# One product order for the tall Strassen-Winograd sets, weight sums into the first block, and x read back on SyncE's queue

## The chip, the cores and the metric

The kernel runs on 1 core of one Trainium2 chip. Times are device microseconds (us). The engines are PE (TensorE, matrix products), ACT (ScalarE), DVE (VectorE), POOL (GpSimd) and SP (SyncE, which here only issues transfers). A share or a wait comes from one profiled execution; the median comes from runs without a profile.

## The reference

One block on x of 512 x 1024 in fp32: a gated feed-forward layer, a mixer, a second feed-forward layer and a norm.

```python
def swiglu(x, w_gu, w_down):
    g, u = jnp.split(x @ w_gu, 2, axis=-1)
    return (jax.nn.silu(g) * u) @ w_down
...
    # mixer, h is the normed x
    z = h @ w_in        # parts cb, cc, cu, q, k, v, g_lr, r, ga, gb
    y_conv = (cb * causal_short_conv(cc * cu, conv_w)) @ w_out_conv
    ...                 # o: gated linear attention of q, k, v, normed by head
    y_gla = (o.astype(h.dtype) * jax.nn.silu(r)) @ w_out_gla
    merged = jax.nn.sigmoid(ga) * y_conv + jax.nn.sigmoid(gb) * y_gla
    return merged @ w_o
...
        x = x + 0.5 * swiglu(rmsnorm(x, norm_ffn1_g[l]), ffn1_w_gu[l], ffn1_w_down[l])
        x = x + hybrid_mixer(rmsnorm(x, norm_mix_g[l]), w_in[l], ...)
        x = x + 0.5 * swiglu(rmsnorm(x, norm_ffn2_g[l]), ffn2_w_gu[l], ffn2_w_down[l])
    return rmsnorm(x, final_norm_g)
```

The hidden width of the feed-forward layers is 2816, which is 22 tiles of 128.

## The kernel before

Every product is done in three passes on split operands: a weight block `f` (128 x 1024 fp32) is cast by ACT to a high part `wh` (L387), DVE subtracts it from the block for the low part `wl` (L388), and PE adds op_high·wh, op_high·wl and op_low·wh. The activations are split in the same way into `op`. Three `wh`, three `wl`, fourteen `op` and ten `f` buffers go round.

Most of the large products use the Strassen-Winograd scheme, seven half-size products for eight, named m1, p2, p5, q6, q7, p4 and p3. The weight block of each is a sum of the four quarters a11, a12, a21, a22. The sums are made in the quarters' own buffers: POOL issues transfers that add one buffer to another (`add`, L354), and DVE does the sum that is called s3 (L381 in tall sets, L366 in the narrow ones). Two kinds of sets use the scheme. A narrow "set" has one weight block for each product. A "tall" set has the inner dimension in two halves, s = 0 and 1, with four quarters each, so it has fourteen steps of twelve 128x512 products (L711). In the SP order, a tall set's quarters are loaded as a11, a21, a22, a12.

A tall set has three pairs of PSUM banks: b takes m1, q6, q7 and p4 one upon another, a starts as a copy of m1 and takes p2, c takes p5 and then p3. What is needed of a sum on the way is copied out after the product's second half: in a feed-forward tall, ACT takes p2 through Silu (L831), p5 (L834), and copies q6 (L837); DVE takes q7 (L839). q7 adds into b, so it can't start before the copy of q6 is done. The first step of the set that follows a tall is put ahead of that tall's p3, and takes the pair a as soon as p2 was read.

The order of the products of a tall is a list. TALL_ORDER is m1, p5, q6, p2, q7, p3, p4; FIRST is m1, p5, p2, q6, q7, p3, p4. The tall sets are, in the order of time: ffn1 up at f = 4, 8, 12 (TALL_ORDER) and 16 (FIRST), each f being the first of four tiles of the hidden width; in the mixer v, ga, gb (TALL_ORDER) and "out", the product with w_out_conv (FIRST); ffn2 up at f = 0 (FIRST), 6, 10, 14, 18 (TALL_ORDER); two of ffn2's down product (DOWN_ORDER). PE's order is that of the code. A scheduler sets the order on the other engines; a step's weights are issued two steps ahead of its products.

In ffn1 and ffn2, sixteen small ACT copies for each of some tall sets (L880, 32x512, from `z` into `hid`) turn the finished tile; they stand between the casts.

Ahead of the last part of the mixer, the attention's output O has been split into operands (L1757, L1758). Then come the two halves e = 0 and 1 of the product with w_out_gla (L459 to L461, eight weight blocks each), and w_o. The gates ga and gb lie in device memory and come back by SP tile by tile (L1770), followed by a sigmoid on ACT (L1771). x, which was written to `xs` earlier, is read back into the buffer that O had (X2), by eight transfers that POOL issues (L1797); w_o's evacuation adds it. SP also issues all weight loads (L350), in one order.

The kernel starts with fp32 products of a 128x128 tile of ones (L283), WARM of them, whose result is not used, each run by PE in two passes.

Of the kernel before, what the change touches and what calls it, by code (L numbers as in the profile page):

```python
# [12 lines left out]
ALU = mybir.AluOpType  # L13
ENG = mybir.EngineType

P = 128
S = 512
D = 1024
KD = D // P
DFF = 2816  # L20
KF = DFF // P
# [13 lines left out]

V_G1, V_GM, V_G2, V_GLA, V_CONV, V_GB = 0, 8, 16, 24, 32, 56
NVEC = 60
WARM = 8
ODD_FILL = 272

TAIL = 4
# [84 lines left out]
LATE = []  # L126
# [5 lines left out]

TALL_ORDER = ("m1", "p5", "q6", "p2", "q7", "p3", "p4")
DOWN_ORDER = ("m1", "p2", "q6", "p5", "q7", "p3", "p4")
FIRST = ("m1", "p5", "p2", "q6", "q7", "p3", "p4")
TALL = {}
ORDERS = {}


def tall(name, mat, cols, base=0, order_=TALL_ORDER):  # L140

    ORDERS[name] = order_

    firsts = []
    for s in range(2):
        firsts.append(len(PLAN))
        TALL[len(PLAN)] = name, s
        PLAN.extend((mat, base + 4 * j + 2 * s, 2, (c,), 512) for c in cols for j in range(2))
    STEPS.extend((n, p) for p in order_ for n in firsts)
# [14 lines left out]
def up_plan(up, plain, slow):  # L164

    kinds = ["tall"] * ((KF - plain) // 4)
    kinds.insert(len(kinds) if slow else 1, "set")
    f = plain
    for kind in kinds:
        if kind == "tall":  # L170
            edge = f == KF - 6 if slow else f == 0
            tall((up, f), up, (f * P, DFF + f * P), order_=FIRST if edge else TALL_ORDER)
        else:
            at = len(STEPS)
            sets(up, [(f * P, DFF + f * P)])
            LATE.append(STEPS[-1][0])
            STEPS[at - 4 : at + 1] = [STEPS[at], *STEPS[at - 4 : at]]
        UPS.setdefault(up, []).append((kind, f))
        f += 4 if kind == "tall" else 2
# [24 lines left out]
def mixer_plan():  # L204
    units(group("w_in", KD, (QO, KO, QO + P, KO + P)))
    for h in (2, 3):
        units(single("w_in", KD, QO + h * P))
        units(single("w_in", KD, KO + h * P))
    for name, col in (("v", VO), ("ga", GA), ("gb", GB)):
        tall(name, "w_in", (col, col + 512))  # L210
    at = len(STEPS)
    base = {"cb": CB, "r": RO}
    sets("w_in", [(CC + i * HW, CU + i * HW) if n == "conv" else
                  (base[n] + 2 * i * HW, base[n] + (2 * i + 1) * HW) for n, i in MSETS])
    LATE.append(STEPS[-1][0])
    STEPS[at - 2 : at + 2] = [STEPS[at], *STEPS[at - 2 : at], STEPS[at + 1]]
    tall("out", "w_out_conv", (0, 512), order_=FIRST)
    for e in range(2):
        units(wide("w_out_gla", KD, 512 * e))
    units(group("w_o", KD, (0, P, 2 * P, 3 * P)))  # L220
    for d in range(4, KD):
        units(single("w_o", KD, d * P))
    ENDS.append(len(STEPS))
# [13 lines left out]
def block_kernel(ctx: ExitStack, tc: tile.TileContext, xT, vecs, gf, gup, wgl, wts, out):  # L237
    nc = tc.nc
# [54 lines left out]
    x = [XS[0][:, k] for k in range(KD)]  # L293
# [3 lines left out]
    class Weights:  # L297
# [58 lines left out]
        def issue(self):  # L356
            at = self.issued
            self.fetch(at)
            new = self.loads.get(at, ())
            raw = {(n, i): self.dma(n + i) for i in ((0, 2, 3, 1) if new and new[0] in TALL else range(4))  # L360
                   for n in new}
            self.raw.update((n, [raw[n, i] for i in range(4)]) for n in new)
            for n in self.sums.get(at, ()):
                self.raw[n].append(tile_of("f", [P, 1024]))
                a11, a12, a21, a22, s3 = self.raw[n]
                nc.vector.tensor_tensor(out=s3, in0=a11, in1=a21, op=ALU.add)  # L366
                self.add(a21, a22)
            for n in self.firsts.get(at, ()):
                self.add(self.raw[n][2], self.raw[n][3])
            for n in self.pre.get(at, ()):  # L370
                self.raw[n] = self.dma(n)
            n, p = STEPS[at]
            w = unit_cols(PLAN[n])
            if p is None:
                raw = self.raw[n]
            else:
                a11, a12, a21, a22, s3 = (self.raw[n] + [None])[:5]
                if n in TALL:
                    if p == "q7":
                        s3 = a11 if ORDERS[TALL[n][0]] == FIRST else a21  # L380
                        nc.vector.tensor_tensor(out=s3, in0=a11, in1=a22, op=ALU.subtract)  # L381
                raw = {"m1": a11, "p2": a12, "q6": a11, "p5": a21, "q7": s3, "p4": a22,
                       "p3": a11 if n in LATE else a12}[p]
            late = at >= len(STEPS) - TAIL
            h = tile_of("op" if late else "wh", [P, 1024], F32R)
            l = tile_of("op" if late else "wl", [P, 1024], F32R)
            nc.scalar.copy(h[:, :w], raw[:, :w])  # L387
            nc.vector.tensor_tensor(out=l[:, :w], in0=raw[:, :w], in1=h[:, :w].bitcast(F32),  # L388
                                    op=ALU.subtract)
            if p == "m1":  # L390
                self.add(a11, a21)
            if n in LATE:
                if p == "q6":
                    self.add(a11, a12)
            elif p == "p2":
                self.add(a12, a11)
            self.issued += 1
            self.ready.append((h, l))
# [398 lines left out]
    def begin_weighed(hid, norm):  # L797
        f = KF - KD
        for k in range(KD):
            nc.scalar.activation(hid[:, f + k], x[k], AF.Copy, scale=norm.g(k))  # L800
        return Operands(lambda j, l: hid[:, f + 4 * j : f + 4 * j + 4, l * HW : (l + 1) * HW],
                        FIRST)

    def ffn(up, down, norm, nxt, plain, at):
        hid = tile_of("hid", [P, KF, S])
# [464 lines left out]
    def mixer(norm, nxt):  # L1270
        xh, xl = norm.h, norm.l
        cpool = pools["small"]
        xs = dram.tile([KD, P, S], F32, tag="xs", name="xs")
# [338 lines left out]
        def split_o(h):  # L1612
            for a, b in split_pair(O[h]):
                og_h.append(a)
                og_l.append(b)
# [21 lines left out]
            (4, "q6"): [lambda: output(3)], (4, "p3"): [lambda: squares(3)],  # L1637
            (5, "q7"): [lambda: normalise(0)], (5, "p3"): [lambda: normalise(1)],
            (6, "q7"): [lambda: normalise(2)], (6, "p3"): [lambda: normalise(3)],
            ("out", 1, "q6"): [lambda: co.make("p4")], ("out", 0, "q7"): [lambda: split_o(0)],  # L1640
            ("out", 1, "q7"): [lambda: split_o(1)], ("out", 0, "p3"): [lambda: split_o(2)],
            ("out", 1, "p3"): [lambda: split_o(3)],
        }
# [146 lines left out]

        def between(e):
            def extra(k):
                if e == 1 and k == 3:
                    XS.append(big("X2"))
                    x[:] = [XS[-1][:, k] for k in range(KD)]
                    for k_ in range(KD):
                        nc.gpsimd.dma_start(x[k_], xs[k_])  # L1797
                if k in (1, 3, 4, 6):
                    t = (1, 3, 4, 6).index(k)
                    mul(m[e][t], m[e][t], gate("ga", t, e))  # L1800
                if e == 1 and k in (5, 6):
                    turned(2 * (k - 5))
            return extra
# [95 lines left out]
```

## Time and profile before

| | before |
|---|---|
| median of 3 runs | 1164.95 us (1162.81 to 1165.26) |
| profiled execution | 1166.64 us |
| its span, first to last instruction | 1164.9 us |
| mean granted TensorE clock | 0.995 |
| PE busy | 1148.0 us |
| DVE, ACT, POOL busy | 895.5, 714.6, 160.3 us |
| moved by DMA | 203.20 MB, mean 174 GB/s |

The span leaves out what lies around the first and the last instruction. A busy share is an average over all stages; the rows below are of single stages. In a row of the trace stand the start, the time, the engine, the line, the operation, out<-in, and the number of instructions; the bracket gives the engine's idle time ahead of it and what ended it.

### The profile page before, as it was taken

Reading aid. Unit: us, or ns where it says so; the run is one execution under the profiler, and the core shown is the slowest. Engines: PE = TensorE matmul, PEld = TensorE weight load, DVE = VectorE, ACT = ScalarE, POOL = GpSimd, SP = SyncE. Lnnn points to the kernel's source line nnn. Section 1 sums busy time; section 2 is a strip of 40 time slices with the busy share of each in tenths; the row PEclk is TensorE's granted clock in tenths of the full one; section 3 lists DMA queues with packets and bytes.
Section 4 is the critical chain, followed back from the end, with each engine's and each line's share of the span. In section 5 each row is a group of like instructions: output and inputs, shape, how many; then the busy total and the mean of one; then the engine's idle time right before and its main releaser. Section 6 shows DMA issues by size and latency. Waiting matters only on the chain.

```text
span 1164.9 us, 16337 instructions
## 1 busy us (share of the span) xinstructions
PE 1148.0 (99%) x6280; PEld 997.7 (86%) x6280; DVE 895.5 (77%) x1061; ACT 714.6 (61%) x923; POOL 160.3 (14%) x199
## 2 busy tenths in 40 slices
PE   9999998999999999999999999999999999999997
PEld 7888787989998888889999998788889878888886
DVE  7986765898887975767797999455876776799966
ACT  6568767755553756665665567524668587665543
POOL 0011111001121010111011112000110464111100
PEclk9999998999999999999999999999999999999999
DMA  9476696557674285788576787834576856877711
GB/s 362 109 198 136 175 246 149 165 135 189 163 217 154 55 237 137 205 235 229 134 172 147 197 205 195 304 109 127 121 170 153 233 145 154 228 202 181 178 55 73
DMA packets 59869, 203.20 MB, mean 174 GB/s; under 512 B 6960, under 2 KB 7088, under 8 KB 59792
## 3 DMA queue, kind: packets, MB, share of 16 engines
q0 software_dynamic: 20288, 73.41, 33.5%
q1 hardware_dynamic: 36912, 124.04, 30.5%
q10 hardware_dynamic: 2592, 4.72, 1.1%
q8 instruction: 49, 0.80, 0.3%
q14 instruction: 28, 0.23, 0.1%
HBM read 124.55 MB, written 8.39 MB: 114 GB/s over the span
## 4 chain that ended last, share of the span: by engine, by line
PE 87%; ACT 6%; DVE 3%; DMA 2%; issue 1%; SPq 0%; ACTq 0%; DVEq 0%
PE mm L711 39%; PE mm L624 24%; PE mm L442 6%; PE mm L420 3%; PE mm L419 3%; PE mm L418 3%; ACT wh L387 3%; ACT hid L880 2%; DVE wl L388 1%; PE mm L460 1%; PE mm L461 1%; PE mm L459 1%; DMA tp<-ga 1%; PE mm L1161 1%; PE mm L1159 1%
## 5 line engine op out<-in xcount | busy, mean ns | idle before, releaser
L388 DVE TENSOR_TENSOR wl<-f,wh 128x1024 fp32r<-128x1024 f32 (+1 forms) x349 | 425.0, 1222 | 172.4 <-ACT wh L387 167.6
L387 ACT CAST wh<-f 128x1024 fp32r<-128x1024 f32 (+1 forms) x349 | 364.4, 1048 | 308.8 <-PE mm L711 103.5
L711 PE MATMUL mm<-wh,op 128*128 128x512 f32 x1680 | 526.3, 392 | 4.7 <-ACT tp L837 3.9
L711 PEld LDWEIGHTS mm<-wh,op 128*128 128x128 f32 x1680 | 316.9, 189 | 71.7 <-ACT tp L837 4.8
L711 PE MATMUL mm<-wl,op 128*128 128x512 f32 x840 | 329.4, 392 | 3.6 <-DVE wl L388 3.3
L624 PE MATMUL mm<-op,wh 128*128 128x256 f32 x1456 | 263.2, 284 | 0.0
L354 POOL DMA_DIRECT2D f<-f x132 | 113.9, 868 | 874.7 <-DVE wl L388 416.4
L624 PEld LDWEIGHTS mm<-op,wh 128*128 128x128 f32 x1456 | 227.6, 192 | 0.7
L624 PE MATMUL mm<-op,wl 128*128 128x256 f32 x728 | 206.3, 283 | 0.0
L711 PEld LDWEIGHTS mm<-wl,op 128*128 128x128 f32 x840 | 158.5, 189 | 39.6 <-DVE wl L388 7.5
L624 PEld LDWEIGHTS mm<-op,wl 128*128 128x128 f32 x728 | 139.6, 192 | 0.0
L880 ACT COPY hid<-z 32x512 f32<-32x512 f32 x112 | 69.2, 618 | 2.8 <-DVE z L874 1.1
L682 ACT CAST op<-hid 128x1024 fp32r<-128x1024 f32 x42 | 44.0, 1050 | 20.3 <-PE mm L711 11.2
L683 DVE TENSOR_TENSOR op<-hid,op 128x1024 fp32r<-128x1024 f32 x42 | 51.1, 1220 | 4.4 <-ACT op L682 4.2
L419 PE MATMUL mm<-op,wh 128*128 128x512 f32 x132 | 51.4, 390 | 0.0
L418 PE MATMUL mm<-op,wh 128*128 128x512 f32 x132 | 51.4, 390 | 0.0
L420 PE MATMUL mm<-op,wl 128*128 128x512 f32 x132 | 51.4, 389 | 0.0
L442 PE MATMUL mm<-op,wh 128*128 128x512 f32 x192 | 48.9, 397 | 0.4 <-DVE op L491 0.4
L381 DVE TENSOR_TENSOR f<-f,f 128x1024 f32<-128x1024 f32 x30 | 37.9, 1269 | 12.9 <-DMA f<-f 6.6
L442 PEld LDWEIGHTS mm<-op,wh 128*128 128x128 f32 x192 | 36.6, 192 | 8.3 <-ACT wh L387 0.6
L1059 POOL COPY X<-hid 32x512 f32<-32x512 f32 x32 | 33.2, 1038 | 1.3
L419 PEld LDWEIGHTS mm<-op,wh 128*128 128x128 f32 x132 | 24.8, 188 | 5.1
(331 smaller groups left out, 1192.5 us busy)
## 6 DMA issues: line engine op xcount, KB each, us to landing
f<-wts SPq DMA_DIRECT2D x219, 512.0 KB, 4.9
f<-f POOLq DMA_DIRECT2D x132, 512.0 KB, 5.2
xs<-X POOLq DMA_DIRECT2D x8, 256.0 KB, 4.4
ga<-tp ACTq DMA_DIRECT2D x8, 256.0 KB, 6.0
gb<-tp ACTq DMA_DIRECT2D x8, 256.0 KB, 5.1
tp<-ga SPq DMA_DIRECT2D x8, 256.0 KB, 5.4
X<-xs POOLq DMA_DIRECT2D x8, 256.0 KB, 7.9
tp<-gb SPq DMA_DIRECT2D x8, 256.0 KB, 5.3
```

The costliest lines, as they stand in the source:

```text
L354: nc.gpsimd.dma_start(out_, a, accum_op=ALU.add)
L387: nc.scalar.copy(h[:, :w], raw[:, :w])
L388: nc.vector.tensor_tensor(out=l[:, :w], in0=raw[:, :w], in1=h[:, :w].bitcast(F32), op=ALU.subtract)
L418: nc.tensor.matmul(o, wh, ah, start=first, stop=False)
L419: nc.tensor.matmul(o, wh, al, start=False, stop=False)
L420: nc.tensor.matmul(o, wl, ah, start=False, stop=last)
L442: nc.tensor.matmul(o[c], w[:, s : s + P], a[k], start=k == 0 and j == 0, stop=k == kt - 1 and j == 2)
L624: nc.tensor.matmul(to, ww[:, s], aa[:, t], start=fresh and k == 0 and e == 0 and j == 0, stop=k == 3 and j == 2, skip_group_check=True)
L682: nc.scalar.copy(hv, v)
L683: nc.vector.tensor_tensor(out=lv, in0=v, in1=hv.bitcast(F32), op=ALU.subtract)
L711: nc.tensor.matmul(self.bank[b][e], aa[:, c], ww, start=fresh and i == 0 and n == 0, stop=k == 3 and n == 2, skip_group_check=True)
L880: nc.scalar.copy(dst[:, :, :, 32 * a : 32 * (a + 1)], src[:, :, :, 32 * q : 32 * (q + 1)])
```

## The change

It has four parts. WARM goes from 8 to 10. FIRST is gone, and the three tall sets that had it use TALL_ORDER, with one hook of "out" moved so that the operand of p4 is still made after the fourth product. In tall sets of TALL_ORDER (`soon`), the subtraction s3 = a11 − a22 is issued at q6 instead of at q7 and always goes into a21, the transfer a11 += a12 is issued behind q6 in place of a12 += a11 behind p2, and p3 reads a11 instead of a12; the down product's tall sets now put s3 into a11. x is read back by SP, one tile with each weight block of w_out_gla's second half.

```diff
-WARM = 8
+WARM = 10
...
-FIRST = ("m1", "p5", "p2", "q6", "q7", "p3", "p4")
...
-            edge = f == KF - 6 if slow else f == 0
-            tall((up, f), up, (f * P, DFF + f * P), order_=FIRST if edge else TALL_ORDER)
+            tall((up, f), up, (f * P, DFF + f * P))
...
-    tall("out", "w_out_conv", (0, 512), order_=FIRST)
+    tall("out", "w_out_conv", (0, 512))
...
                 a11, a12, a21, a22, s3 = (self.raw[n] + [None])[:5]
+                soon = n in TALL and ORDERS[TALL[n][0]] == TALL_ORDER
                 if n in TALL:
-                    if p == "q7":
-                        s3 = a11 if ORDERS[TALL[n][0]] == FIRST else a21
+                    s3 = a21 if soon else a11
+                    if p == "q7" and not soon:
                         nc.vector.tensor_tensor(out=s3, in0=a11, in1=a22, op=ALU.subtract)
                 raw = {"m1": a11, "p2": a12, "q6": a11, "p5": a21, "q7": s3, "p4": a22,
-                       "p3": a11 if n in LATE else a12}[p]
+                       "p3": a11 if soon or n in LATE else a12}[p]
...
             if p == "m1":
                 self.add(a11, a21)
-            if n in LATE:
+            if p is not None and (soon or n in LATE):
                 if p == "q6":
+                    if soon:
+                        nc.vector.tensor_tensor(out=s3, in0=a11, in1=a22, op=ALU.subtract)
                     self.add(a11, a12)
             elif p == "p2":
                 self.add(a12, a11)
...
-            ("out", 1, "q6"): [lambda: co.make("p4")], ("out", 0, "q7"): [lambda: split_o(0)],
+            ("out", 1, "p2"): [lambda: co.make("p4")], ("out", 0, "q7"): [lambda: split_o(0)],
...
-                if e == 1 and k == 3:
+                if e == 1 and k == 0:
                     XS.append(big("X2"))
                     x[:] = [XS[-1][:, k] for k in range(KD)]
-                    for k_ in range(KD):
-                        nc.gpsimd.dma_start(x[k_], xs[k_])
+                if e == 1:
+                    tc.keep_in_program_order(nc.sync.dma_start(x[k], xs[k]))
```

ACT's order at ffn1 f = 16, before. mm234 and mm235 are the banks b, with q6, and mm240 and mm241 the banks a, with p2; f213 and f221 are a11 of the two halves, here holding s3 of q7.

```order
L831 ACTIVATE tp258_1558<-mm240_1468 128x512
L880 COPY hid20_188<-z229_1390 32x16x32
L831 ACTIVATE tp259_1560<-mm241_1469 128x512
L387 CAST wh260_1565<-f213_1298 128x1024
L880 COPY hid20_188<-z229_1390 32x16x32 x2
L387 CAST wh263_1587<-f221_1343 128x1024
L880 COPY hid20_188<-z229_1390 32x16x32
L837 COPY tp265_1603<-mm234_1430 128x512
L837 COPY tp266_1605<-mm235_1431 128x512
```

The same place after (L838 is L837 of before, L832 is L831, L386 is L387, and L881 is L880; f214 and f222 are a21):

```order
L838 COPY tp258_1562<-mm234_1432 128x512
L881 COPY hid20_190<-z229_1392 32x16x32
L838 COPY tp259_1564<-mm235_1433 128x512
L386 CAST wh260_1568<-f214_1302 128x1024
L881 COPY hid20_190<-z229_1392 32x16x32 x2
L386 CAST wh263_1589<-f222_1347 128x1024
L881 COPY hid20_190<-z229_1392 32x16x32
L832 ACTIVATE tp265_1605<-mm240_1470 128x512
L832 ACTIVATE tp266_1607<-mm241_1471 128x512
```

The copies of q6 and the evacuation of p2 have changed places; the casts of q7's two halves stand between them as before.

DVE's order in the same tall, from the split of p5's second half on, before (f213 to f216 are a11, a21, a22 and a12 of the first half, f221 to f224 those of the second):

```order
L388 TENSOR_TENSOR wl239_1453<-f222_1345,wh238_1452 128x1024
L388 TENSOR_TENSOR wl249_1485<-f216_1304,wh248_1484 128x1024
L388 TENSOR_TENSOR wl251_1503<-f224_1349,wh250_1502 128x1024
L388 TENSOR_TENSOR wl255_1526<-f213_1298,wh254_1525 128x1024
L381 TENSOR_TENSOR f213_1298<-f213_1298,f215_1302 128x1024
L388 TENSOR_TENSOR wl257_1543<-f221_1343,wh256_1542 128x1024
L381 TENSOR_TENSOR f221_1343<-f221_1343,f223_1347 128x1024
```

And after (L387 is L388 of before, L394 is L381):

```order
L387 TENSOR_TENSOR wl239_1455<-f222_1347,wh238_1454 128x1024
L394 TENSOR_TENSOR f214_1302<-f213_1300,f215_1304 128x1024
L394 TENSOR_TENSOR f222_1347<-f221_1345,f223_1349 128x1024
L387 TENSOR_TENSOR wl249_1487<-f213_1300,wh248_1486 128x1024
L387 TENSOR_TENSOR wl251_1506<-f221_1345,wh250_1505 128x1024
L387 TENSOR_TENSOR wl255_1530<-f216_1306,wh254_1529 128x1024
L387 TENSOR_TENSOR wl257_1547<-f224_1351,wh256_1546 128x1024
```

Both subtractions now stand ahead of the splits of q6, directly behind p5's; in f = 8 and f = 12 they stood there before too.

SP's order at the second half of w_out_gla, before (f1043, f1047 and f1055 are blocks of weights, the tp tiles the gates):

```order
L350 DMA f1039_7093<-wts 128x1024
L1770 DMA tp1042_7123<-ga_3187 128x512
L350 DMA f1043_7127<-wts 128x1024
L1770 DMA tp1046_7166<-ga_3187 128x512
L350 DMA f1047_7170<-wts 128x1024
L1770 DMA tp1050_7188<-ga_3187 128x512
```

And after (L348 is L350, L1771 is L1770):

```order
L348 DMA f1039_7095<-wts 128x1024
L1798 DMA X2_7113<-xs_3188 128x512 x2
L1771 DMA tp1042_7128<-ga_3189 128x512
L348 DMA f1043_7132<-wts 128x1024
L1798 DMA X2_7113<-xs_3188 128x512 x2
L1771 DMA tp1046_7164<-ga_3189 128x512
L348 DMA f1047_7168<-wts 128x1024
L1798 DMA X2_7113<-xs_3188 128x512
L1771 DMA tp1050_7187<-ga_3189 128x512
L1798 DMA X2_7113<-xs_3188 128x512
```

The eight reads of x stand between gates and weights, the other two behind the block after these; in POOL's order the row of eight behind the last sum of "out" is gone.

More of the change, by code (lines that the diff above doesn't have):

```diff
@@ L801, in begin_weighed @@
         return Operands(lambda j, l: hid[:, f + 4 * j : f + 4 * j + 4, l * HW : (l + 1) * HW],
-                        FIRST)
+                        TALL_ORDER)
     def ffn(up, down, norm, nxt, plain, at):
```

## The prediction

> **What bounds the kernel now.** I read the page's first two parts, then what TensorE waits for, then the stretch around each wait in order of time.
>
> ```profile
> span 1164.9 us, 16337 instructions
> PE 1148.0 (99%) x6280; PEld 997.7 (86%) x6280; DVE 895.5 (77%) x1061; ACT 714.6 (61%) x923; POOL 160.3 (14%) x199
> ```
>
> TensorE (PE) is busy 99% of the span. The products stay the same but for two more at the start, so the change can only act on TensorE's few gaps and on stretches of low clock. Its waits, but for two at the start:
>
> ```profile
> PE mm L711 <- ACT tp L837: 3.9, 2, 3.2
> PE mm L711 <- DVE wl L388: 3.3, 6, 0.8
> PE mm L460 <- DVE wl L388: 0.8, 1, 0.8
> PE mm L711 <- ACT wh L387: 0.7, 1, 0.7
> ```
>
> Columns: total us, times, longest. These are 8.7 us in ten waits. L711 is the products of the tall sets, L460 those of w_out_gla. The first row's two waits are the two ffn talls in the FIRST order: q7 adds into the bank that L837 must first copy q6 out of. The longer of them, ffn1 f=16, TensorE's rows and then ScalarE's (ACT):
>
> ```profile
> 188.20 0.62 PE L711 MATMUL mm<-wh,op 128*128 128x512 f32 x2
> 188.88 0.39 PE L711 MATMUL mm<-wh,op 128*128 128x512 f32 x1
> 192.51 0.80 PE L711 MATMUL mm<-wh,op 128*128 128x512 f32 x1 [3.25 <-ACT tp L837]
> 198.23 0.51 PE L711 MATMUL mm<-wl,op 128*128 128x512 f32 x1
> ...
> 187.82 1.05 ACT L387 CAST wh<-f 128x1024 fp32r<-128x1024 f32 x1
> 188.90 1.24 ACT L880 COPY hid<-z 32x512 f32<-32x512 f32 x2
> ...
> 191.88 1.07 ACT L837 COPY tp<-mm 128x512 f32<-128x512 f32 x2
> ```
>
> The pitch of such products is 0.227 us (188.20 to 188.88 is three of them). q6's last product starts at 188.88, q7's first at 192.51, while ScalarE works from 187.82 to 191.88 through casts and copies that stand ahead of L837 in its order. After the wait the clock is down:
>
> ```profile
> 192.50:198.20 5.70, 5.69 (x13) 4.48 (x14) 1.25 (x2) 1.65 (x3) 0.26 (x2) 0.50 0.85 184
> ```
>
> The column behind the five engines is the granted clock: 0.50, with TensorE busy all the time.
>
> **The change, part by part.**
>
> *FIRST to TALL_ORDER at ffn1 f=16.* p2 (two halves of 12 products, 5.4 us at 0.227) now stands between q6 and q7, and L837 takes the place in ScalarE's order that p2's L831 had, ahead of the casts above. What such a tall does, the trace shows in f=8:
>
> ```profile
> 106.72 0.59 ACT L837 COPY tp<-mm 128x512 f32<-128x512 f32 x1
> 107.84 0.57 ACT L837 COPY tp<-mm 128x512 f32<-128x512 f32 x1
> 109.96 0.61 PE L711 MATMUL mm<-wh,op 128*128 128x512 f32 x2
> 110.80 0.50 PE L711 MATMUL mm<-wl,op 128*128 128x512 f32 x1 [0.22 <-DVE wl L388]
> 111.13 0.62 PE L711 MATMUL mm<-wh,op 128*128 128x512 f32 x2
> ```
>
> The copies end at 108.41, q7 starts two products before 110.4 and doesn't wait for them; it waits 0.22 us for a weight split. The gain at f=16 from start to start: 192.51 − 188.88 − 0.23 = 3.40 for the wait; 13 products from 192.51 to 198.23 took 5.72 instead of 13 × 0.227 = 2.95, 2.77 for the clock; together 6.2. What f=8 has left at this place I take off: 111.13 − 109.96 = 1.17 for three products of 0.68, so 0.49. **−5.7 us**; at least −2.9 (the wait without the clock), at most −6.2.
>
> The Trainium skill ("TensorE: Matmul & The Clock Gate", Part 1: The HAM clock gate) says that the clock falls to half after an idle window of about 3.4 us and returns after a busy one, with windows that run freely. The rows show the fall after an idle time of 3.25 us, below that figure; by the rule to the letter this wait would leave the clock up, and the sum would lose the 2.77.
>
> *The same order at ffn2 f=0 and at "out".* In ffn2 f=0:
>
> ```profile
> 852.26 0.39 PE L711 MATMUL mm<-wh,op 128*128 128x512 f32 x1
> 852.71 1.08 ACT L837 COPY tp<-mm 128x512 f32<-128x512 f32 x2
> 853.35 0.51 PE L711 MATMUL mm<-wh,op 128*128 128x512 f32 x1 [0.70 <-ACT tp L837]
> ```
>
> 853.35 − 852.26 − 0.23 = **−0.9**, with 5.4 us of p2 as the new cover; at least 0 if p2's own evacuation takes its place, at most 0.9. At "out" no wait stands in the list, and none goes.
>
> *Weight sums.* a11 += a12 starts behind q6's split and not behind p2's, and p3 reads a11. The subtraction a11 − a22 (DVE, 1.23 us) moves from ahead of q7's split to ahead of q6's where it did not stand there already: f=4, f=16, "out", ffn2 f=0. No instruction is added. What may gain is the next tall's loads: a12 is no longer written behind p2, so it comes free at p2's split, where so far SyncE's load waited until the sum into a12 had landed. In f=12 and f=16 the chain behind those late loads reaches TensorE:
>
> ```profile
> 109.62 12.11 SPq L350 DMA_DIRECT2D f<-wts  x8
> 125.47 1.75 POOL L354 DMA_DIRECT2D f<-f  x2 [9.61 <-DVE tp L593]
> 131.06 1.05 ACT L387 CAST wh<-f 128x1024 fp32r<-128x1024 f32 x1 [2.74 <-DMA f<-f]
> 136.53 1.23 DVE L381 TENSOR_TENSOR f<-f,f 128x1024 f32<-128x1024 f32 x1 [1.42 <-DMA f<-f]
> 138.95 0.50 PE L711 MATMUL mm<-wl,op 128*128 128x512 f32 x1 [0.66 <-DVE wl L388]
> ```
>
> The eight loads begin at 109.62. In f=8, p2 began two half-steps before q7's 109.96 + 0.23, at 104.7, and its split was done by then; so the first of them may go 4.9 us earlier. ScalarE's stall of 2.74 us for a sum then shrinks, and the 0.66 before TensorE goes. But f=16 now takes q6 directly behind p5, as f=12 does, and so the subtraction ahead of its split can cost it what f=12 pays: between −1.3 (twice the 0.66) and +0.7 (f=16 as f=12, and nothing gained). Nearest is f=12's own row, gone with its stall: **−0.7**. In the mixer's talls no wait of TensorE stands in the list; I give them nothing, the cover being splits that end ahead of their products.
>
> *x read back.* Before, all eight loads leave POOL together once O is free:
>
> ```profile
> 721.97 4.31 POOL L1797 DMA_DIRECT2D X<-xs  x8 [12.43 <-DVE op L1758]
> X<-xs POOLq DMA_DIRECT2D x8, 256.0 KB, 7.9
> 719.00:742.00 23.00, 20.73 (x88) 15.97 (x87) 13.85 (x16) 13.53 (x18) 4.31 (x8) 1.00 0.96 347
> 742.00:765.00 23.00, 23.00 (x104) 19.03 (x103) 13.52 (x17) 9.97 (x15) 0.00 (x0) 1.00 0.62 202
> 732.56 0.63 ACT L1771 ACTIVATE tp<-tp 128x512 f32<-128x512 f32 x1 [5.68 <-DMA tp<-ga]
> 734.18 0.50 PE L711 MATMUL mm<-wh,op 128*128 128x512 f32 x1 [0.75 <-ACT wh L387]
> 735.44 0.50 PE L711 MATMUL mm<-wl,op 128*128 128x512 f32 x1 [0.76 <-DVE wl L388]
> 739.23 0.50 PE L460 MATMUL mm<-wl,op 128*128 128x512 f32 x1 [0.76 <-DVE wl L388]
> ```
>
> The last two columns of a window are the DMA share and GB/s. From 719 to 742 the engines are full (0.96, 347 GB/s); a gate tile that ScalarE's order puts ahead of casts arrives late, ScalarE stands 5.68 us, and TensorE waits 0.75 + 0.76 + 0.76 = 2.27. The eight tiles are 2.1 MB, 91 GB/s of those 347; without them some 256 are asked. In the new place, the window 742 to 765, they make 202 + 91 = 293 GB/s, below the 347. On SyncE they put eight issues ahead of gates and weights. ScalarE's cover there:
>
> ```profile
> 761.10 1.05 ACT L387 CAST wh<-f 128x1024 fp32r<-128x1024 f32 x1 [4.38 <-PE mm L461]
> ```
>
> it waits 4.38 us for TensorE to free a weight buffer, so weights are that much ahead. At most all 2.27 go, at least none (the gate loads are late by themselves, or the stall moves to the second half). With 256 GB/s asked of 347 no backlog is left in the first window, so I take most of it: **−2.0**. x itself is used only by w_o's evacuations, behind 784.
>
> The Trainium skill ("DMA: Bandwidth & Descriptors", Issuing engines are not separate DMA queues) speaks against a gain from the queue alone: all issuers share the same 16 engines. By it, SyncE instead of POOL is worth only issue time, and what counts is that the loads leave 20 us later; the 2.0 rests on that shift.
>
> *Warming.*
>
> ```profile
> 1.11 3.79 PE L283 MATMUL aux<-ones 128*128 128x128 f32 x16 [1.11 <-POOL ones L280]
> 5.27 3.03 PE L442 MATMUL mm<-op,wh 128*128 128x512 f32 x8 [0.37 <-DVE op L491]
> 8.14 1.08 PE L442 MATMUL mm<-op,wl 128*128 128x512 f32 x4
> ```
>
> Eight products took 3.79 (0.474 each), and so ten end at 1.11 + 4.74 = 5.85: the 0.37 gap is filled and the first real product is 0.58 late. The first eight real ones took 2.87 start to start (8 × 0.227 = 1.82), so they lose 1.05 at the low clock; a later start makes fewer of them slow, and about half of the 0.58 comes back: **+0.3**, between −0.5 (full clock from the first on) and +0.6.
>
> *New waits elsewhere* (f=4's two subtractions ahead of a split, the last down product's in-place ones, regrouped ScalarE rows): nothing in the list waits there now; 0 to two waits of 0.76, and by the empty list nearer to 0: **+0.3**.
>
> **Sum.** −5.7 − 0.9 − 0.7 − 2.0 + 0.3 + 0.3 = −8.7. The profiled execution took 1166.64 (1.7 around its span of 1164.9): 1157.9. The median is 1164.95 and so 1.7 lower: 1156.3. I predict **1156.3**. All ends together give −11.2 and −0.1; one run of before lies at 1162.81, 2.1 below the median, which is near the 2.77 of the clock. Faster, same and slower are told apart at 0.2%, 2.3 us.
>
> **Rivals.**
>
> 1. *The clock.* In ordinary runs the clock stays up at 192 (it would explain 1162.81). Against it: two of three runs lie with the profiled one. Then 2.8 of the gain are missing: 1159.1.
>
> 2. *The evacuation that moves back takes the wait* (the change does not do what it says). At f=16 p2's L831 now stands where L837 stood, 191.88 to 192.95, and frees the bank that the f=20 set's first product needs. TensorE reaches that product 5.4 us behind p2. By the rows p2 would end at 188.88 + 0.39, q7 5.4 later at 194.7, so 1.7 us are to spare. If ScalarE is later by 1.7 + 3.25, wait and clock come back and the 5.7 is gone: 1162.0.
>
> 3. *The reads collide again.* In w_out_gla's second half the gates wait behind x on SyncE and stop ScalarE as at 732.56. The cover of 4.38 speaks against. The 2.0 is gone, 1158.3; a stop as long as the 5.68 would pass on 1.3 more, 1159.6.
>
> 4. *Slower: the subtraction ahead of q6's split.* DVE is in order, and the subtraction waits for a POOL sum to land (1.42 us at 136.53, with 0.66 for TensorE behind it). a11's sum now stands ahead of the next tall's sums in POOL's order, so these could land later. If the stall grows from f=12's by 2.6 us, TensorE's idle time reaches 3.25 and each such tall costs 6.2 with the clock. One tall eats most of the gain (1162.5); from two on it is slower: −8.7 + 2 × 6.2 = +3.7, 1168.7. For it: the chain is tight in f=12 and f=16. Against: the sum is issued some 5 us earlier than the one it replaces.
>
> **How the numbers follow.** My forecast, with its own range 1153.5 to 1158.5: 0.60. Rival 1: 0.12; rival 2: 0.07; rival 3: 0.13; rival 4: 0.08, half of it with one tall. Faster by over 0.2% (below 1162.6) are the forecast, rivals 1 and 3, most of 2 and some of one-tall 4: 0.89; within: 0.06; slower: 0.05. From 1153.0 to 1161.5 the range takes in the forecast and rivals 1 and 3 with 0.83 of the chance, a little of it off at the ends.
>
> **What would show it.** Right: TensorE waits no more for L837, no low clock near 192, the f=16 tall's q7 like f=8's; no stop at a gate near 732 and the first w_out_gla products at pitch; the first real product near 5.9. Wrong: a wait of the f=20 set for L831's copy or of q6 for DVE at f=16; a stop at a gate near 750; DMA share near 0.96 in the second half; a new wait in a tall that had none.

## The result, and the profile after

| | before | after |
|---|---|---|
| median | 1164.37 us (1162.81 to 1165.26, 6 runs) | 1155.97 us (1155.78 to 1157.19, 6 runs) |
| profiled execution | 1166.64 us | 1157.14 us |
| its span | 1164.9 us | 1155.4 us |
| mean granted clock | 0.995 | 0.999 |

The ratio is 0.9932, with a 95% interval of 0.992 to 0.9945: 8.4 us faster between the medians, 9.5 between the profiled executions. 1156.3 had been forecast. The sum came out; two of the reasons in it did not, and one wait is new. One run of all those below, of the kernel with the order alone, took 1257.82 us at a mean granted clock of 0.851 and is left out of the comparisons.

What TensorE waits for in the changed kernel (total us, times, longest; L712 is L711 of before, L625 is L624, both one or a few lines off as all lines are):

```profile
PE mm L712 <- DVE wl L387: 1.8, 5, 0.7
PE mm L625 <- ACT tp L633: 1.3, 1, 1.3
PE aux L281 <- POOL ones L278: 1.1, 1, 1.1
```

Of the 8.7 us in ten waits of before 3.1 in six are left, and 1.3 of them are new. No wait for the copy of q6 is there any more. ffn1 f=16, TensorE at q7 and ScalarE beside it (the row at 187.76 holds p2's last product and q7's first, which starts at 187.99):

```profile
187.76 0.61 PE L712 MATMUL mm<-wh,op 128*128 128x512 f32 x2
188.60 0.50 PE L712 MATMUL mm<-wl,op 128*128 128x512 f32 x1 [0.22 <-DVE wl L387]
191.72 0.61 PE L712 MATMUL mm<-wh,op 128*128 128x512 f32 x2
...
184.51 0.59 ACT L838 COPY tp<-mm 128x512 f32<-128x512 f32 x1
185.64 0.57 ACT L838 COPY tp<-mm 128x512 f32<-128x512 f32 x1
190.30 1.08 ACT L832 ACTIVATE tp<-mm 128x512 f32<-128x512 f32 x2
...
187.90:194.00 6.10, 5.88 (x27) 4.49 (x26) 4.51 (x5) 5.40 (x8) 0.86 (x1) 1.00 0.38 75
```

The copies (L838) are done 1.8 us ahead of q7, what remains is the 0.22 that f=8 has too, and the granted clock in the window is 1.00 where it was 0.50.

Where the 9.5 us come from is read by taking the start of the same product in both traces. The difference, after less before, at places where it jumps:

| place | before | after | difference | step |
|---|---|---|---|---|
| 81st real product | 24.51 | 25.07 | +0.6 | +0.6 |
| f=12, q6 | 138.95 | 138.71 | −0.2 | −0.8 |
| f=16, second product behind p5 (q6 before, p2 after), first half | 183.76 | 182.78 | −1.0 | −0.7 |
| f=16, q7's second half | 198.58 | 191.72 | −6.9 | −5.9 |
| f=20 set, behind p2 | 226.15 | 221.12 | −5.0 | +1.8 |
| "out", end | 719.54 | 714.53 | −5.0 | 0.0 |
| w_out_gla | 739.56 | 731.30 | −8.3 | −3.3 |
| ffn2 f=0, q7 | 853.69 | 844.43 | −9.3 | −1.0 |
| end of the span | 1164.9 | 1155.4 | −9.5 | −0.2 |

The +1.8 is the new wait. The narrow set f=20 follows f=16. Its rows after, of SyncE, DVE, POOL, ScalarE and TensorE:

```profile
182.16 2.68 SPq L348 DMA_DIRECT2D f<-wts  x2
188.58 1.23 DVE L364 TENSOR_TENSOR f<-f,f 128x1024 f32<-128x1024 f32 x1
190.33 0.86 POOL L352 DMA_DIRECT2D f<-f  x1 [11.25 <-ACT hid L881]
197.22 0.86 POOL L352 DMA_DIRECT2D f<-f  x1 [6.03 <-DVE wl L387]
205.25 1.05 ACT L386 CAST wh<-f 128x1024 fp32r<-128x1024 f32 x1 [4.39 <-PE mm L712]
214.66 1.88 ACT L881 COPY hid<-z 32x512 f32<-32x512 f32 x3 [2.41 <-DVE z L875]
220.49 0.58 ACT L633 COPY tp<-mm 128x512 f32<-128x512 f32 x1
221.12 0.50 PE L625 MATMUL mm<-op,wh 128*128 128x256 f32 x2 [1.32 <-ACT tp L633]
```

and before:

```profile
173.55 3.14 SPq L350 DMA_DIRECT2D f<-wts  x2
190.17 1.22 DVE L366 TENSOR_TENSOR f<-f,f 128x1024 f32<-128x1024 f32 x1
191.69 0.86 POOL L354 DMA_DIRECT2D f<-f  x1 [11.04 <-DVE f L366]
197.99 0.86 POOL L354 DMA_DIRECT2D f<-f  x1 [5.44 <-issue]
```

TensorE reaches this set 6 us earlier, but the set's weights don't: its last two loads start 8.6 us later (173.55 to 182.16), since p2 comes later. Its first sum on DVE stands behind the split of f=16's q7, and that is paced by ScalarE's casts and copies: it starts 1.6 us earlier (190.17 to 188.58), and the two sums by POOL behind it 1.4 and 0.8. The second of these starts at 197.22 and lands at 205.15, 7.9 us later; before it landed after 4.8 us, at 202.79, and q6's cast came only at 209.39. The DMA share between the start and the landing is 0.95, before it was 0.74. At 205.25 the cast of q6 begins; DVE and the copies L881 run late behind it, and the copy L633 of the set's q7 with them. So 1.8 of the 5.9 us were given back by a chain that had 6 us of cover from the wait itself. The row at 205.25 names TensorE as what released the cast; by the landing 0.1 us ahead of it I read the sum as the cause, as the same cast's row in another kernel below does.

For x, SyncE's rows and two windows (behind the clock: DMA share, GB/s):

```profile
728.25 2.36 SPq L1798 DMA_DIRECT2D X<-xs  x2
742.34 0.43 SPq L1798 DMA_DIRECT2D X<-xs  x1
731.34 1.37 ACT L1772 ACTIVATE tp<-tp 128x512 f32<-128x512 f32 x2 [2.80 <-DMA tp<-ga]
719.00:742.00 23.00, 23.00 (x103) 19.02 (x103) 14.49 (x17) 13.43 (x19) 0.00 (x0) 1.00 0.95 323
742.00:765.00 23.00, 23.00 (x103) 19.06 (x102) 11.34 (x15) 8.83 (x11) 0.00 (x0) 1.00 0.63 216
```

The DMA share from 719 to 742 is 0.95, as it was (0.96), and seven of the eight reads start in it. But ScalarE's longest stop at a gate is 2.80 us in place of 5.68, and TensorE is busy in all 23 us.

### The profile page after: what moved, and what is told of

The parts are those of the page before. It is cut to its first block, busy times and chain, and to the rows that moved or that the text cites. A ratio compares the mean times of both kernels' runs of the same rounds, so it can differ in the third digit from the quotient of the medians.

```text
span 1155.4 us, 16314 instructions
## 1 busy us (share of the span) xinstructions
PE 1144.6 (99%) x6284; PEld 996.3 (86%) x6284; DVE 893.9 (77%) x1061; ACT 714.7 (62%) x923; POOL 149.5 (13%) x191
## 4 chain that ended last, share of the span: by engine, by line
PE 90%; ACT 6%; DVE 2%; issue 1%; ACTq 0%; POOL 0%; POOLq 0%
PE mm L712 42%; PE mm L625 24%; PE mm L443 6%; PE mm L421 3%; PE mm L419 3%; PE mm L420 3%; ACT wh L386 3%; ACT hid L881 2%; PE mm L461 1%; PE mm L460 1%; PE mm L462 1%; DVE wl L387 1%; PE mm L1161 1%; PE mm L1160 1%; PE mm L1162 1%
## 5 line engine op out<-in xcount | busy, mean ns | idle before, releaser
L387 DVE TENSOR_TENSOR wl<-f,wh 128x1024 fp32r<-128x1024 f32 (+1 forms) x349 | 424.5, 1221 | 173.2 <-ACT wh L386 168.2
L386 ACT CAST wh<-f 128x1024 fp32r<-128x1024 f32 (+1 forms) x349 | 364.3, 1048 | 297.5 <-PE mm L712 94.8
L712 PE MATMUL mm<-wh,op 128*128 128x512 f32 x1680 | 522.9, 390 | 0.0
L712 PEld LDWEIGHTS mm<-wh,op 128*128 128x128 f32 x1680 | 315.4, 188 | 65.2
L712 PE MATMUL mm<-wl,op 128*128 128x512 f32 x840 | 327.7, 390 | 1.9 <-DVE wl L387 1.8
L625 PE MATMUL mm<-op,wh 128*128 128x256 f32 x1456 | 263.4, 283 | 1.3 <-ACT tp L633 1.3
L625 PEld LDWEIGHTS mm<-op,wh 128*128 128x128 f32 x1456 | 227.4, 192 | 2.3 <-ACT tp L633 1.5
L625 PE MATMUL mm<-op,wl 128*128 128x256 f32 x728 | 206.1, 283 | 0.1
L712 PEld LDWEIGHTS mm<-wl,op 128*128 128x128 f32 x840 | 157.7, 188 | 36.9 <-DVE wl L387 4.7
L625 PEld LDWEIGHTS mm<-op,wl 128*128 128x128 f32 x728 | 139.4, 191 | 0.3 <-DVE wl L387 0.3
L881 ACT COPY hid<-z 32x512 f32<-32x512 f32 x112 | 69.3, 618 | 5.6 <-DVE z L875 3.9
L394 DVE TENSOR_TENSOR f<-f,f 128x1024 f32<-128x1024 f32 x26 | 31.8, 1234 | 7.1 <-issue 4.3
L421 PEld LDWEIGHTS mm<-op,wl 128*128 128x128 f32 x132 | 24.8, 188 | 5.4 <-DVE wl L387 0.3
```

The costliest lines, as they stand in the source:

```text
L421: nc.tensor.matmul(o, wl, ah, start=False, stop=last)
L625: nc.tensor.matmul(to, ww[:, s], aa[:, t], start=fresh and k == 0 and e == 0 and j == 0, stop=k == 3 and j == 2, skip_group_check=True)
L712: nc.tensor.matmul(self.bank[b][e], aa[:, c], ww, start=fresh and i == 0 and n == 0, stop=k == 3 and n == 2, skip_group_check=True)
L881: nc.scalar.copy(dst[:, :, :, 32 * a : 32 * (a + 1)], src[:, :, :, 32 * q : 32 * (q + 1)])
```

## The experiments

**The order alone.** The kernel before, with the lists changed (and with them the hook of "out" and one argument that names the list) and nothing else:

```diff
-            tall((up, f), up, (f * P, DFF + f * P), order_=FIRST if edge else TALL_ORDER)
+            tall((up, f), up, (f * P, DFF + f * P))
...
-    tall("out", "w_out_conv", (0, 512), order_=FIRST)
+    tall("out", "w_out_conv", (0, 512))
...
```

> The kernel before with TALL_ORDER at the three tall sets and nothing else. Theory (the copy of q6 was late because it stood behind casts and copies in ScalarE's order, and its lateness cost the clock too): TensorE's waits for that copy go at ffn1 f=16 (5.8 us) and ffn2 f=0 (0.9); the last two loads of the f=20 set come later, since p2 comes later in f=16, and its q6 waits (1.9 us or somewhat more, as the changed kernel shows 0.37 and 1.48). Together about -4.8: 1159.6 us against 1164.4. Rival (p2's evacuation takes the wait over): a wait at the f=20 set's first product and 1163 to 1164. Second rival (the wait at the f=20 set comes from the new weight sums): no such wait here, 1157.7.

Measured: 1169.36 us against 1164.78, ratio 1.0048 (1.003 to 1.0066): slower, which neither the theory nor a rival had. The copy's wait is gone here too. The f=20 set shows why it doesn't pay:

```profile
185.83 0.86 POOL L353 DMA_DIRECT2D f<-f  x1 [1.48 <-DVE wl L387]
188.14 4.15 SPq L349 DMA_DIRECT2D f<-wts  x3
192.70 1.23 DVE L365 TENSOR_TENSOR f<-f,f 128x1024 f32<-128x1024 f32 x1 [0.77 <-DMA f<-wts]
201.26 0.86 POOL L353 DMA_DIRECT2D f<-f  x1 [5.18 <-DVE wl L387]
208.22 1.05 ACT L386 CAST wh<-f 128x1024 fp32r<-128x1024 f32 x1 [6.35 <-DMA f<-f]
```

With the old sums a12 is written behind p2, and p2 now comes later; the set's last loads wait until that lands and start at 188.14, 6 us later than in the changed kernel. The set's first sum waits for them, the second starts at 201.26, and q6's cast 3 us later than there. TensorE's waits at the set are 0.39, 0.76, 0.39 and 1.33 us, and the set behind ffn2 f=0 has two of over 1 us. The starts of the same products in this trace and in that of before say it in sum: f=16's q7 gains 5.5 us and ffn2 f=0 0.9, the f=20 set takes 3.9 back and the set behind ffn2 f=0 3.7. The two profiled executions lie 1.9 us apart and the medians 4.6; where the other 2.7 come from no trace shows. The theory on the copy held; its price did not.

**The weight sums alone** (the two hunks on `soon` of the change, FIRST kept).

> The kernel before with the new weight sums in the tall sets of TALL_ORDER, FIRST kept where it was. Theory (loads come earlier by the early release of a12): ScalarE's waits of 2.74 and 3.32 us for a sum at f=12 and f=16 go, TensorE's 0.66 at f=12 and its late splits at f=16 go, -1.5 us: 1162.9. Rival (these small waits come from ScalarE's backlog of copies, not from the sums): less than 0.4 us, 1164.2.

Measured: 1163.77 against 1164.78, ratio 0.9993 (0.9983 to 1.0004): not told from no change. In its trace the waits at f=12's q6 and at f=16's steps behind p5 are gone, as expected. At the gates ScalarE's longest stop is about as long as before (5.3 us against 5.7), but TensorE waits 2.5 us there in place of 2.3 and the clock falls, which takes 2 us of the gain back in this trace.

**Order and sums together**, without the other two parts.

> The kernel before with TALL_ORDER at the three tall sets and the new weight sums, x still read by POOL and 8 warming products. Alone the order cost 4.8 us and the sums gained about 1. If the two need each other (the order puts the release of a12, and with it the next set's last loads, behind p2, and only the new sums keep that release from waiting for a sum to land there): the changed kernel's time and the stop at the gates on top, 2.9 to 5 us: 1159 to 1161. If they act independently: 1164.4 + 4.8 - 1.0 = 1168.

Measured: 1161.7 against 1164.72, ratio 0.9968 (0.9956 to 0.998). Alone +4.6 and −1.0, together −3.0: the two need each other, as the loads' rows say. The gain is a little less than expected (1159 to 1161). Between the medians 5 us are left to the changed kernel, more than the 3 that x gives alone (below). The two profiled executions lie 2.7 us apart: 2.9 at the gates and 1.1 behind them, less 1.2 ahead of them. How the rest of the 5 us comes about stays open.

**FIRST back at f=16 in the changed kernel.**

```diff
...
+                 order_=FIRST if slow and f == KF - 6 else TALL_ORDER)
```

> The changed kernel with FIRST back at ffn1 f=16 alone (with the weight sums that go with it). If the terms add: the wait and the low clock come back (5.8), the late splits at f=16 too in part (up to 0.9), and the wait at the f=20 set goes (1.9): 1156.0 + 4 to 5 = 1160 to 1161. If the wait at the f=20 set has nothing to do with the order: 1162.

Measured: 1158.49 (1156.35 to 1158.67), 2.5 above the changed kernel's 1155.97, less than expected. By the ratios to before, 0.9946 (0.9933 to 0.9959) and 0.9932, it is 1.6, and the intervals overlap. Here is its profiled run, the fastest of the five, and then the same place in the kernel with the sums alone, both with a wait of 2.8 us:

```profile
189.66 0.50 PE L714 MATMUL mm<-wh,op 128*128 128x512 f32 x1 [2.81 <-ACT tp L840]
184.95:188.37 3.42, 1.90 (x9) 1.24 (x7) 2.28 (x2) 3.33 (x4) 0.00 (x0) 1.00 0.00 0
188.37:191.78 3.41, 2.12 (x9) 1.77 (x10) 1.88 (x3) 2.74 (x4) 0.86 (x1) 1.00 0.57 96
191.78:195.00 3.22, 3.22 (x15) 2.65 (x15) 1.84 (x3) 1.05 (x1) 0.00 (x0) 1.00 0.92 223
```

```profile
189.85 0.50 PE L714 MATMUL mm<-wh,op 128*128 128x512 f32 x1 [2.80 <-ACT tp L840]
186.89:190.31 3.42, 0.62 (x3) 0.42 (x3) 2.94 (x3) 3.32 (x6) 0.86 (x1) 1.00 0.00 0
190.31:193.72 3.41, 3.41 (x10) 2.63 (x9) 1.23 (x1) 1.04 (x1) 0.00 (x0) 0.50 1.04 161
```

The same idle time left the clock at 1.00 in one run and at 0.50 for 3.41 us in the other. The traces show where the difference lies. In all fourteen of them the granted clock changes only at whole multiples of 3.413 us after the moment at which it first comes up, which is 4 to 10 us after the start (4.05 with FIRST back, 5.99 with the sums alone). The windows shown are cut at these steps. With FIRST back one step ends in the middle of the wait, so that 1.52 us of it lie in one step and 1.29 in the next. With the sums alone all 2.80 lie in one step, and in the step behind it the clock is at half.

Counted over all steps of the fourteen traces: behind a step in which TensorE stood without a product for 1.79 us or more the clock was always at half; behind one with 1.51 or less it never fell. Three steps lie between, and one of them brought the clock down: two waits of 0.77 and 0.76 us at the gates with the sums alone. So it is not the length of one wait that counts, but the idle time within one step, and where the steps lie differs from run to run.

The four other runs of this kernel took 1158.05 to 1158.67 us at a mean granted clock of 0.997, the profiled one 1156.35 at 0.998. One step at half clock costs 1.7 us and would make that difference, but for those four no trace is on record, so it is not shown. The set at f=20 has no wait in this kernel, as the terms said.

The Trainium skill ("TensorE: Matmul & The Clock Gate", Part 1: The HAM clock gate) says that the windows in which activity is counted run freely, so that the point of a change varies from run to run. These two runs agree with that; its figure of 3.4 us of idle time does not hold as a bound here, since 2.80 us were enough once, and two waits of 0.77 and 0.76 us another time.

**Work in the gap.** In the kernel before, twelve products of the tile of ones between q6 and q7 of f=16:

```diff
+        else:
+            def busy():
+                o = AUX()
+                for i in range(12):
+                    nc.tensor.matmul(o[:, :P], ones, ones, start=True, stop=True)
+            at_step(((up, KF - 6), 1, "q6"), busy)
```

> The kernel before with twelve products of the tile of ones put between q6 and q7 of ffn1 f=16, 2.8 us of work at the full clock, in place of most of TensorE's idle 3.25 us. Nothing else is changed, and q7 still waits for the copy. If the idle time brings the clock down: q7's first half takes 2.7 us and not 5.5, granted clock 1.0 there, -2.8 us: 1161.6. If q7 is slow for another reason, such as the copies beside it or the DMA traffic: no change, 1164.4, or somewhat more if the products of ones run late.

Measured: 1162.85 against 1163.98, ratio 0.9989 (0.998 to 0.9998). The trace is of the slowest of its twelve runs, 1167.20 us:

```profile
187.82 2.84 PE L1001 MATMUL aux<-ones 128*128 128x128 f32 x24
191.24 0.50 PE L711 MATMUL mm<-wh,op 128*128 128x512 f32 x1 [0.58 <-ACT tp L837]
191.58 0.39 PE L711 MATMUL mm<-wl,op 128*128 128x512 f32 x1
191.81 0.62 PE L711 MATMUL mm<-wh,op 128*128 128x512 f32 x2
191.20:197.00 5.80, 5.76 (x26) 4.79 (x27) 2.90 (x4) 2.58 (x3) 0.37 (x2) 1.00 0.85 184
```

q7 starts as late as ever, for the same copy, but at full pitch and at 1.00. Against the trace of before, q7's first half gains 2.8 us. So the idle time is what brings the clock down, and q7's slowness had no other cause; the runs agree, with a mean granted clock of 0.999 in eight of the twelve and of 0.995 to 0.998 in the seventeen of before beside them. The gain of 1.1 between the medians is smaller than the 2.8 forecast. In part the clock falls for different lengths: in six traces with the wait of f=16 (the kernel before, the sums alone, the three kernels for x below, FIRST back) it was at half for two steps in two, for one step in three, and not at all in one. In the trace above 4.6 us are lost again at two other places, the mixer's tall at 505 and the gates; whether the twelve products have to do with that stays open.

**x by SyncE alone**, in the second half as in the change, and then in the first half (`e == 0` in both places):

```diff
-                if e == 1 and k == 3:
+                if e == 1 and k == 0:
...
-                    for k_ in range(KD):
-                        nc.gpsimd.dma_start(x[k_], xs[k_])
+                if e == 1:
+                    tc.keep_in_program_order(nc.sync.dma_start(x[k], xs[k]))
```

> The kernel before with x read back by SyncE, one tile with each k of w_out_gla's second half, and nothing else. Theory: the stop of 5.68 us at a gate near 732 goes and with it TensorE's three waits, 2.9 us from start to start: 1161.4. Rival (the gate loads are late by themselves): waits of 1 us and more stay there, 1163 or more.

> As the one before, but with the eight tiles read in the first half of w_out_gla: SyncE's queue as in the changed kernel, the time as in the kernel before. If the place in time is what helps: the DMA share is again near 0.96 from 719 to 742, ScalarE stops at a gate and TensorE waits 1.5 to 3 us, 1163 to 1165. If SyncE's queue helps (the transfers go in turn with the gates and don't stand as one block ahead of them): no such stop, about 1161.5.

Measured: 1161.96, ratio 0.9975 (0.9964 to 0.9987), and 1161.73, ratio 0.9974 (0.9964 to 0.9984), against 1164.78. Neither has a wait of TensorE there. The early one, from 727 to 742:

```profile
727.00:742.00 15.00, 15.00 (x67) 12.40 (x67) 9.71 (x11) 9.72 (x14) 0.00 (x0) 1.00 1.03 392
```

The DMA share is 1.03, no less than in the kernel before (1.02, in a row further below), and TensorE is busy throughout. So the place in time is not what helps.

**x by POOL, in pairs.** The kernel before, each pair of reads behind a small POOL copy that waits for a gate of the first half:

```diff
...
+                    if e == 0:
+                        tc.keep_in_program_order(nc.gpsimd.tensor_copy(fill[:, t : t + 1], g[:, 0:1]))
+                        for k_ in (2 * t, 2 * t + 1):
+                            tc.keep_in_program_order(nc.gpsimd.dma_start(x[k_], xs[k_]))
```

> The kernel before with x still read by POOL in the first half of w_out_gla, but in four pairs, each behind a 128x1 copy that waits for one of the four ga gates (sigmoid done), in place of eight at once. If the block of eight at once is what held up the gates: no stop over 3 us of ScalarE and no waits of TensorE there, about 1161.7, as with SyncE in either half. If POOL's own queue taking its share beside SyncE's is what held them up: the stop stays, 1163 to 1165.

Measured: 1160.68 against 1164.72, ratio 0.9966 (0.9954 to 0.9978), and no wait there. The kernel before and then this one:

```profile
727.00:742.00 15.00, 12.73 (x54) 9.68 (x53) 8.00 (x9) 6.77 (x10) 0.00 (x0) 1.00 1.02 373
727.00:742.00 15.00, 15.00 (x68) 12.43 (x67) 7.79 (x10) 8.76 (x13) 5.13 (x9) 1.00 1.02 379
```

The queue is not what helps either. What cost 3 us is that eight reads were issued in one block, ahead of the gates; spread between them, on SyncE's queue at either time or on POOL's in the first half, they cost TensorE nothing. (No run issues the block of eight on SyncE's queue.) How much the block costs differs from kernel to kernel. The window from 727 to 742 in the kernels with the order, the sums, both, and the work in the gap:

```profile
727.00:742.00 15.00, 11.98 (x50) 8.77 (x49) 7.53 (x9) 7.60 (x12) 0.00 (x0) 1.00 0.99 368
```

```profile
727.00:742.00 15.00, 12.50 (x44) 9.09 (x44) 8.73 (x11) 9.97 (x15) 0.00 (x0) 0.89 0.94 352
```

```profile
727.00:742.00 15.00, 13.26 (x56) 10.17 (x56) 9.92 (x11) 9.98 (x15) 0.00 (x0) 1.00 0.93 337
```

```profile
727.00:742.00 15.00, 11.85 (x44) 8.78 (x43) 6.29 (x8) 5.93 (x9) 0.00 (x0) 0.89 0.92 329
```

TensorE (the first number behind the length) is idle 3.0, 2.5, 1.7 and 3.2 of the 15 us, and twice the clock (0.89) goes down with it.

**Eight warming products in the changed kernel.**

> The changed kernel with 8 warming products in place of 10. My theory in the prediction: the two more cost 0.3 us, so 0.3 faster here. By the changed kernel's trace the ninth real product starts within 0.03 us of the kernel before, so: no difference, within 0.3. Rival (the gap between warming and the first real product delays the clock): 0.3 to 0.6 slower here.

Measured: 1157.13 (1155.84 to 1158.32), ratio to before 0.9939 (0.9925 to 0.9952); the changed kernel has 0.9932 and, run again, 0.9934. No difference can be told. Over the profiled runs the 151st real product starts between 39.8 and 41.6 us with eight and between 39.6 and 40.9 with ten: the scatter of the start is larger than what two products do.

**The last sets' loads in another order**, against the new wait at f=20:

```diff
-            raw = {(n, i): self.dma(n + i) for i in ((0, 2, 3, 1) if new and new[0] in TALL else range(4))
+            raw = {(n, i): self.dma(n + i) for i in ((0, 2, 3, 1) if new and (new[0] in TALL or new[0] in LATE) else range(4))
```

> The changed kernel with the quarters of the last narrow sets loaded as a11, a21, a22, a12, as in tall sets, where they were loaded a11, a12, a21, a22. In the changed kernel the f=20 set's last two loads wait for buffers until f=16's p2 is split, and two sums of 6.4 and 7.9 us stand behind them before q6 of that set can be cast. If this is why TensorE waits 0.37 and 1.48 us at that set: a22 comes one load earlier, some 2 us, the first sum too, and the waits get smaller or go: 1154.2 to 1155. If they come from ScalarE's backlog of copies: no change, 1156.0.

Measured: 1154.88 (1154.49 to 1155.43), as expected. Then once more, beside the changed kernel on the same chip:

> The changed kernel once more, on the same chip as the next one: 1156.0, between 1155.5 and 1157.3.

> The changed kernel with a11, a21, a22, a12 as the order of loads in the last narrow sets, once more beside the changed kernel: by the first run's trace the waits at the f=20 set shrink from 1.85 to 0.44, so 1.0 to 1.5 us below the changed kernel, 1154.5 to 1155. If that difference came from the chip or from the scatter of the start: none.

Measured: 1156.89 (1156.5 to 1158.3) and 1154.97 (1154.92 to 1155.2), ratios to before 0.9934 (0.9922 to 0.9946) and 0.9916 (0.9903 to 0.9929). The two sets of runs don't overlap, 1.9 us lie between the medians: this version is faster than the changed kernel and the kernel before. Between the two traces 1.9 of 2.0 us lie at this set. Its rows:

```profile
189.34 0.86 POOL L352 DMA_DIRECT2D f<-f  x1 [11.00 <-DVE f L364]
195.78 0.86 POOL L352 DMA_DIRECT2D f<-f  x1 [5.57 <-DVE tp L840]
203.30 1.05 ACT L386 CAST wh<-f 128x1024 fp32r<-128x1024 f32 x1 [3.19 <-DMA f<-f]
219.17 0.51 PE L625 MATMUL mm<-op,wh 128*128 128x256 f32 x2 [0.48 <-ACT tp L633]
```

The cast of q6 starts 2.0 us earlier than in the changed kernel, 1.2 of it against TensorE (q7 of f=16 was 0.8 earlier too), and the row now names the sum as what it waits for. The first sum started hardly earlier, since DVE's share of it still stands behind q7's split, which waits 2.82 us for ScalarE's cast: the theory of late loads is right in part only, and ScalarE's backlog holds the rest.

## Why the prediction was right, and where it was not

- **f=16, "−5.7 us".** −5.9 in the table, by the mechanism told: the copy ahead of the casts, then the wait and the clock gone. The 2.77 for the clock is borne out by the work in the gap, which gave 2.8 at q7 in its trace. In ordinary runs f=16 may be worth less, since the profile of before is one of two traces in six in which the clock was at half for two steps; FIRST put back cost 1.6 to 2.5, and work in the gap gave 1.1 between medians. Rival 1, which I gave 0.12, is in part true.
- **ffn2 f=0, "−0.9".** −1.0.
- **Weight sums, "−0.7".** −1.5 in the table (f=12 and f=16), beyond the −1.3 that I gave as the end. That is in part the luck of one trace. The kernel with work in the gap and the three for x run the program of before up to there; from the 81st product to the place behind p5 they take 158.1 to 158.5 us, the trace of before 159.3, and all traces with the new sums 157.7. So the sums give 0.4 to 1.5, and 0.7 lies between. (The order alone, with the old sums, takes 157.8, so that not all of it need be theirs.) Both talls came out clean but for 0.22 at q7, with the early loads:

```profile
104.92 2.68 SPq L348 DMA_DIRECT2D f<-wts  x2
130.52 1.06 ACT L386 CAST wh<-f 128x1024 fp32r<-128x1024 f32 x1 [1.62 <-PE mm L712]
```

The first load stood at 109.62 and ScalarE's cast waited for a sum at 131.06. "I give them nothing" and "what may gain" were the wrong frame for this part: its main use is that the new order is possible at all. I had added order and sums as two terms, and they are +4.6 and −1.0 alone, −3.0 together.

- **x, "the 2.0 rests on that shift".** Wrong in the reason and too small, −3.3. The step that failed is "the new place, the window 742 to 765": the reads start at 728, the share stays at 0.95, and the stop goes all the same. "At most all 2.27 go" was too tight as well, since the products at the end of such a wait start at a slower pitch (2.9 from start to start). The Trainium skill ("DMA: Bandwidth & Descriptors", Issuing engines are not separate DMA queues) was right that the queue as such gives no more than issue time; POOL in pairs shows it, at 0.9966 against 0.9975 and 0.9974 for SyncE.
- **Warming, "+0.3".** Nothing that runs can tell. The first real product starts at 5.40 and not "near 5.9", 0.13 us later than before, and the ninth 0.02 earlier; the gap of 0.37 is gone. The table's +0.6 comes behind these, and the second trace of the changed kernel has 24.08 where the table has 25.07.
- **New waits, "+0.3".** +1.8. The failing step is "by the empty list nearer to 0": a list of waits shows what is late while TensorE arrives at its present time. f=16's 6 us of waiting had been cover for the next set, and taking it away was bound to show what was behind it. Rival 2 named this set but looked at its first product and at L831 (L832), which was done at 191.38 and delayed nothing.
- **Rivals 3 and 4.** The reads did collide, without harm. No subtraction made q6 late: f=16's q6 starts at pitch.

Errors of +1.5 (new waits) and −2.1 (x, sums) offset each other in the sum. That the forecast of 1156.3 came so close to 1155.97 is luck to that extent.

## What to carry to other kernels

When a wait goes, ask what used it as cover: follow the next stage's loads, sums and casts back to what starts them, and see whether that moves with TensorE or with another engine. Terms that touch the same buffers are not to be added from separate estimates; build the pairs. Transfers that a later engine waits for in order want the bulk reads spread between them; a full DMA share by itself says little. Short waits that lie close together may cost the clock as one long wait does, and one trace with a low clock in it says little of the other runs.

## What was not expected of the hardware

The granted clock changed only in steps of 3.413 us, and fell behind a step in which TensorE had stood 1.79 us or more, never behind one with 1.51 or less. So it fell after 2.80 us without a product in one run and stayed at 1.00 after 2.81 in another. Where it fell ahead of the kernel's end, it was at half for 3.41 us five times and for 6.83 us twice. Twelve products on a tile of ones kept it up. With the DMA engines at 392 GB/s and a share of 1.03 over 15 us, a TensorE that was fed by them lost nothing.
